# Layer 1's mixer on one Trainium2 core: one Strassen product with 512-column blocks in place of two with 256-column blocks

## The chip, the core and the metric

The kernel runs on one core of a Trainium2 chip. The core has a matrix engine (PE, with its weight loads shown apart as PEld), a vector engine (DVE), a scalar engine (ACT), a general engine (POOL) and a sync engine (SP) that only issues transfers. Operands lie in a memory of 128 partitions; PE writes to eight accumulation banks of 128 x 512 float32 each, which DVE and ACT read. The metric is the device time of one execution in microseconds, lower is better. Before the change it is 975.41 us, the median of three runs (975.31 to 975.7).

## The reference, cut to what matters

Two layers over 512 positions of width 1024. The change lies in the mixer of layer 1:

```python
xn = rms_norm(h, norm_mix[1])
proj = gelu(einsum('bsd,de->bse', xn, w_in_odd[0]))     # 1024 -> 2048
u, v = proj[..., :1024], proj[..., 1024:]
vn = rms_norm(v, sgu_norm)                               # over all 1024 columns of v
gate = einsum('hts,bnshc->bnthc', tril(w_spatial), chunks(vn)) + b_spatial
h = h + einsum('bse,ed->bsd', u * gate, w_out_odd[0])
```

All matrix products are wanted in float32 accuracy.

## The kernel before

**Float32 by three terms.** Every float32 operand is split into a high part `hi` and a rest `lo`, both of the type float32r. A product is `hi*hi + hi*lo + lo*hi`, three matmuls. A weight block is split by `parts` (L149): ACT copies to `hi` (L152), DVE subtracts to `lo` (L153). `summed` (L138) makes `lo` another way: ACT writes the negated copy (L142), a transfer issued by POOL adds the raw weights onto it (L144), and ACT then writes `hi` (L146).

**Buffers.** Raw weights go through four buffers of 128 x 1024 float32 (tag `raw`), which `fetch` (L130) fills from SP's queue (L132). `hi` and `lo` have six buffers of the same size each (tags `whi`, `wlo`). Seven accumulation banks are shared by all products (`mm_bank`), one more (`aux_bank`) by small turns and sums. In the mixer's own pool the tag `vn` has four buffers of 128 x 2048, `v` four of 128 x 1024, `u` two and `ws` one of 128 x 2048.

**The order of instructions.** The program lists instructions in the order of the code; a planner then makes each engine's queue, by priority in that order among what its own cost model says is ready, and gives out buffers in the same pass. So the code of a later step may run ahead of an earlier one. A few instructions are pinned behind the one traced before them on their engine (`inorder`) or behind a named one (`behind`). Once made, each queue is worked off in order, and an instruction that waits holds back all behind it.

**The stage.** `mixer1` (L898) works out 512 positions x 2048 columns from 1024 inputs, in four groups of 512 columns:

1. v's first 512 columns by `v_group` (L905): four position tiles x 8 k blocks x 3 terms, each matmul with a 128 x 128 tile of activations as the stationary operand and a 128 x 512 weight row as the moving one.
2. v's second 512 columns as a Strassen product (Winograd's form), `InProducts("v1", 1536)` (L1045). The activations are cut into halves of positions and of k, the weights into halves of k and of columns (2 x 256). Seven block products take the place of eight. `block_sums` (L946) makes the four sums of activation blocks that products 5, 6, 7 and 3 need; `InProducts.rest` (L992) makes the sums of weight blocks (L995, L997, L999, L1001) and splits them. Each product is, for two position tiles `i`, 4 k blocks x 3 terms (`multiply`, L558, line 581), 128 x 256 wide.
3. u's first 512 columns in the same way, `InProducts("u0", 0)` (L1048).
4. u's second 512 columns by `in_group` (L1145) without Strassen, into which `along` (L1129) weaves the turning of the spatial weights (`turn_spatial`, L1118, whose two turns share the one `aux_bank`), the spatial products (`spatial`, L1069) and the turns of the gated result.

Products gather in banks: 1, 6, 7 and 4 one after the other onto bank `a` of their position tile, 5 and 3 onto bank `e`, 2 in bank `b` (`BANK`, L554). Between them ACT copies the running value out (L1019, L1023), DVE adds the other bank (L1024, L1030), and ACT applies the gelu with the row's norm factor (L1037). In `run` (L1005) the products' order is 1, 1, 2, 2, 6, 6, 5, 7, 5, 7, 4, 3, 4, 3 over the two tiles.

**v's norm.** `v_square` (L931) sums the squares of each half of v by row. `beside_u0` (L1102), run inside u's first product, adds the two sums, takes the inverse root (`newton`, L242, with ACT's root function, L246) and normalises v's first half into `vnh`, `vnl` (`v_normed`, L1053, lines 1058 and 1059, two `vn` buffers). The second half follows after u's first product, into the `vn` buffers that the activation sums held.

Of the kernel before, what the change touches and what calls it, by code (L numbers as in the profile page):

```python
# [8 lines left out]
F32 = mybir.dt.float32  # L9
# [3 lines left out]
ALU = mybir.AluOpType  # L13
PSUM = bass.MemoryType.PSUM

P = 128
# [15 lines left out]
def tile_trunk(ctx: ExitStack, tc: tile.TileContext, x, norm_mix, norm_ffn, final_norm,  # L32
# [3 lines left out]
    nc = tc.nc  # L36
    x = x[0]
# [8 lines left out]
    def mm_bank(name):  # L46
        return ps_mm.tile([P, 512], F32, tag="mm", name=name)
# [82 lines left out]
    def fetch(src, a, b, name):  # L130
        raw = wp.tile([P, a, b], F32, tag="raw", bufs=4, name=f"raw_{name}")
        nc.sync.dma_start(raw, src)  # L132
        return raw, a, b, name
# [124 lines left out]
    def inv_sqrt_cols(ss, n, name):  # L258
        r = tp.tile([P, LINE], F32, tag="rc", name=f"rc_{name}")[:, :n]
        root_ends[name] = inv_sqrt(r, ss, n, name)  # L260
        return r
# [286 lines left out]
    HALF = S // 2  # L548
    NP = NK // 2
# [4 lines left out]
    BANK = {1: "a", 6: "a", 7: "a", 4: "a", 5: "e", 3: "e", 2: "b"}  # L554
# [3 lines left out]
    def multiply(banks, name, product, left, right, both=None):  # L558

        at = BANK[product]
        first = at not in banks
        if first:
            banks[at] = mm_bank(f"{name}{at}")
        ps = banks[at][:, :HALF]
        if both is not None:
            for kp in range(NP):  # L570
                nc.tensor.matmul(banks[at], left(kp)[0], both(kp), start=first and kp == 0,  # L571
                                 stop=kp == NP - 1, skip_group_check=True)
            for kp in range(NP):
                last_matmul[0] = nc.tensor.matmul(ps, left(kp)[1], right(kp)[0], start=False,
                                                  stop=kp == NP - 1, skip_group_check=True)
            return banks[at]
        for kp in range(NP):
            (a_hi, a_lo), (b_hi, b_lo) = left(kp), right(kp)
            for l, r, end in ((a_hi, b_hi, False), (a_hi, b_lo, False),
                              (a_lo, b_hi, kp == NP - 1)):  # L580
                nc.tensor.matmul(ps, l, r, start=first, stop=end, skip_group_check=True)  # L581
                first = False
        return ps
# [314 lines left out]
    def mixer1(norm):  # L898
        w = w_in_odd[0]
        with tc.tile_pool(name="m1", bufs=1) as mp:  # L900
# [27 lines left out]
            banks = v_group(0, {(4, 0): lambda: norm.rstd_cols(inorder)})  # L928
            ssv = mp.tile([P, 4, PAD], F32, name="ssv")[:, :, :NT]

            def v_square(half, t):  # L931
                sq = tp.tile([P, S], F32, tag="sq", name=f"sqv{half}_{t}")
                nc.scalar.activation(sq, v[t][:, half * 512 : (half + 1) * 512], AF.Square,
                                     accum_out=ssv[:, half, t : t + 1])


            sums = [[mp.tile([P, 2, 4, HALF], F32R, name=f"s{q}_{n}", **where)
                     for n, where in enumerate(at)]
                    for q, at in enumerate(((dict(tag="vn", bufs=4),) * 2,
# [22 lines left out]
            def tokens(product, i):  # L962

                def at(kp):
                    if product in SUM:
                        cs = slice(i * P, (i + 1) * P)
                        return tuple(x[:, kp % 2, SUM[product], cs] for x in sums[kp // 2])
                    k = kp if product == 1 else kp + NP
                    cs = slice((i + 2 * (product == 4)) * P, (i + 2 * (product == 4) + 1) * P)
                    return hg[k][0][:, cs], hg[k][1][:, cs]  # L970
                return at

            class InProducts:


                def __init__(self, name, c0):
                    self.name, self.stat = name, {}
                    self.raw = {}
                    for i, j in ((0, 0), (1, 0), (0, 1), (1, 1)):
                        self.raw[i, j] = fetch(  # L980
                            w[i * 512 : (i + 1) * 512, c0 + j * HALF : c0 + (j + 1) * HALF]
                            .rearrange("(k p) c -> p k c", p=P), 4, HALF, f"{name}_{i}{j}")

                def plain(self):
                    self.put(1, parts, (0, 0))
                    self.put(2, summed, (1, 0))

                def put(self, product, how, at):
                    raw, a, b, name = self.raw[at]
                    self.stat[product] = how(raw, a, b, f"{name}_{product}")  # L990

                def rest(self):  # L992
                    b11, b21, b12, b22 = (self.raw[at][0] for at in
                                          ((0, 0), (1, 0), (0, 1), (1, 1)))
                    nc.vector.tensor_tensor(b12, b12, b11, ALU.subtract)  # L995
                    self.put(5, parts, (0, 1))
                    nc.vector.tensor_tensor(b12, b22, b12, ALU.subtract)  # L997
                    self.put(6, parts, (0, 1))
                    nc.vector.tensor_tensor(b11, b12, b11, ALU.subtract)  # L999
                    self.put(7, parts, (0, 0))  # L1000
                    nc.vector.tensor_tensor(b21, b21, b12, ALU.subtract)  # L1001
                    self.put(4, parts, (1, 0))
                    self.put(3, parts, (1, 1))

                def run(self, out_, done, behind_first):  # L1005
                    banks = ({}, {})
                    e = {}
                    for i, product in ((0, 1), (1, 1), (0, 2), (1, 2), (0, 6), (1, 6), (0, 5),
                                       (0, 7), (1, 5), (1, 7), (0, 4), (0, 3), (1, 4), (1, 3)):
                        if (i, product) == (0, 2):  # L1010
                            behind_first()
                        hi, lo = self.stat[product]
                        ps = multiply(banks[i], f"{self.name}_{i}", product, tokens(product, i),
                                      lambda kp: (hi[:, kp, :], lo[:, kp, :]))
                        c = {1: (0, 0), 2: (0, 0), 6: (0, 1), 3: (0, 1), 7: (1, 1), 5: (1, 1),
                             4: (1, 0)}[product]
                        dst = out_(i + 2 * c[0])[:, c[1] * HALF : (c[1] + 1) * HALF]
                        if product in (1, 6):
                            nc.scalar.copy(dst, ps)  # L1019
                        elif product == 5:  # L1020
                            e[i] = ps
                        elif product == 7:
                            nc.scalar.copy(dst, ps)  # L1023
                            nc.vector.tensor_tensor(dst, e[i], dst, ALU.add)  # L1024
                            gelu(dst, dst, i + 2)
                        elif product == 4:
                            gelu(dst, ps, i + 2)
                            done(i + 2)
                        else:
                            nc.vector.tensor_tensor(dst, ps, dst, ALU.add)  # L1030
                        if product == 3:
                            row = out_(i)
                            gelu(row, row, i)
                            done(i)

            def gelu(dst, src, t):
                nc.scalar.activation(dst, src, AF.Gelu, scale=norm.cols[:, t : t + 1])  # L1037
# [3 lines left out]
            v = [mp.tile([P, D], F32, tag="v", bufs=4, name=f"v{t}") for t in range(NT)]  # L1041
            for t in range(NT):
                gelu(v[t][:, :512], banks[t], t)
                v_square(0, t)
            v1 = InProducts("v1", 1536)  # L1045
            v1.plain()
            v1.run(lambda t: v[t][:, 512:], lambda t: v_square(1, t), v1.rest)
            u0 = InProducts("u0", 0)  # L1048
            u0.plain()

            vn, rv = [], []

            def v_normed(half):  # L1053
# [10 lines left out]
            u, gt, mix = {}, {}, {}  # L1064
# [34 lines left out]

            u[0] = mp.tile([P, NT, S], F32, tag="u", bufs=2, name="u0")  # L1100

            def beside_u0():  # L1102
                nc.vector.tensor_tensor(ssv[:, 0, :], ssv[:, 0, :], ssv[:, 1, :], ALU.add)
                rv.append(inv_sqrt_cols(ssv[:, 0, :], NT, "v"))
                v_normed(0)
                u0.rest()

            u0.run(lambda t: u[0][:, t, :], lambda t: None, beside_u0)

            v_normed(1)  # L1110
            ws = wp.tile([P, NK, P], F32, tag="raw", bufs=4, name="ws")
            nc.scalar.dma_start(ws, w_spatial[0].rearrange("h t s -> t h s"))
# [286 lines left out]
    n = mixer0()  # L1399
    n = ffn0(n)  # L1400
    n = mixer1(n)
    ffn1(n)

# [29 lines left out]
```

## Time and profile before

| what | value |
|---|---|
| median of three runs | 975.41 us |
| the profiled execution's span | 973.0 us |
| mean granted PE clock | 0.998 |
| v's first half (v_group), start | 485.29 us |
| the two Strassen products, first to last start | 508.00 to 548.24 us |
| u's second half, start | 548.36 us |
| output projection (oo), start | 578.47 us |

Times are counted from the span's start. The span runs from the first to the last instruction of one profiled execution. A row of a timeline has the start, the duration, the engine, the line, the operation and the tiles as out<-in, their shape, the count of merged instructions and, in brackets, how long the engine was idle before it and what ended that. The duration of one matmul is longer than the step to the next, since matmuls are pipelined; the pace is read from start to start. Windows list each engine's busy time with the number of instructions, the granted clock, the share of the transfer engines and their rate.

### The profile page before, as it was taken

The page shows a single profiled execution, that of the slowest core. Times are in us where ns is not written, and L with a number is a line of the kernel's source. Part 1 is how long each engine was busy: PE and PEld are TensorE (multiplying, and loading weights), DVE is VectorE, ACT ScalarE, POOL GpSimd, SP SyncE. Part 2 cuts the span into 40 slices and gives each one's busy share as a digit, 9 for nine tenths or more (in the row PEclk, how much of TensorE's full clock was granted, in tenths as well). Part 3 has the DMA queues.
Part 4 walks back from the last instruction along what each step waited for, and adds up shares of the span by engine and source line. Part 5 has one row for each costly group of instructions (what it writes and reads, how often), then busy time and mean ns, then how long its engine had stood idle before and what let it go on. Part 6 is the DMA issues. An engine that isn't in the chain of part 4 may idle for free.

```text
span 973.0 us, 14003 instructions
## 1 busy us (share of the span) xinstructions
PE 963.6 (99%) x5120; PEld 828.8 (85%) x5120; DVE 817.0 (84%) x1393; ACT 598.7 (62%) x905; POOL 149.9 (15%) x173
## 2 busy tenths in 40 slices
PE   9999999999999999999999999999999999999996
PEld 7888888988888888888889988889888888888885
DVE  5887458999899898998986865589998989889897
ACT  5523347765676665765487734587765667656775
POOL 2142023110111010110310001221111011100123
PEclk9999999999999999999999999999999999999999
DMA  7442225776777677774324623167767777668775
GB/s 251 146 139 86 87 88 108 178 178 165 195 178 181 146 178 185 174 174 140 119 58 110 221 67 99 55 132 187 186 145 194 196 173 172 156 165 201 194 153 140
DMA packets 94417, 148.36 MB, mean 152 GB/s; under 512 B 5156, under 2 KB 60428, under 8 KB 94348
## 3 DMA queue, kind: packets, MB, share of 16 engines
q1 hardware_dynamic: 78316, 98.69, 32.2%
q0 software_dynamic: 14256, 46.93, 26.7%
q10 hardware_dynamic: 1776, 1.84, 0.6%
q8 instruction: 40, 0.66, 0.3%
q14 instruction: 29, 0.24, 0.1%
HBM read 98.42 MB, written 2.10 MB: 103 GB/s over the span
## 4 chain that ended last, share of the span: by engine, by line
PE 99%; DVE 1%; issue 0%; ACT 0%; POOLq 0%; DVEq 0%; POOL 0%
PE dn L158 3%; PE d L158 3%; PE dn L159 3%; PE dn L157 3%; PE d L159 3%; PE d L157 3%; PE gu L157 2%; PE gu L159 2%; PE oo L159 1%; PE oo L157 1%; PE gu L158 1%; PE oe L157 1%; PE oe L159 1%; PE oo L158 1%; PE oe L158 1%; PE u_2a L581 1%
## 5 line engine op out<-in xcount | busy, mean ns | idle before, releaser
L617 DVE SCALAR_TENSOR_TENSOR c<-rows,prm,c 128x512 f32<-128x512 f32 x88 | 65.6, 748 | 1.5 <-ACT c L615 1.4
L144 POOL DMA_DIRECT2D wlo_g<-raw_g x20 | 17.2, 860 | 321.3 <-DVE kept L804 187.4
L158 PE MATMUL dn<-wlo_dn,a_hi 128*128 128x512 f32 x144 | 56.3, 391 | 0.0
L158 PE MATMUL d<-a_lo,whi_d 128*128 128x512 f32 x144 | 56.3, 391 | 0.0
L159 PE MATMUL dn<-whi_dn,a_lo 128*128 128x512 f32 x144 | 56.2, 391 | 0.0
L159 PE MATMUL d<-a_hi,wlo_d 128*128 128x512 f32 x144 | 56.2, 390 | 0.0
L157 PE MATMUL d<-a_hi,whi_d 128*128 128x512 f32 x144 | 56.2, 390 | 0.0
L157 PE MATMUL dn<-whi_dn,a_hi 128*128 128x512 f32 x144 | 56.2, 390 | 0.0
L731 ACT ACTIVATE whi_a<-raw_g 128x512 fp32r<-128x512 f32 x20 | 12.6, 631 | 61.0 <-PE g_10e L571 8.7
L213 POOL TENSOR_TENSOR ssq_f<-ssq_f,sq_f 128x512 f32<-128x512 f32 x14 | 19.8, 1411 | 134.4 <-ACT sq_f L212 99.5
L202 ACT ACTIVATE hg<-h,prm 128x512 fp32r<-128x512 f32 x24 | 17.3, 722 | 34.9 <-DVE h L315 34.9
L142 ACT ACTIVATE wlo_g<-raw_g 128x1024 fp32r<-128x1024 f32 x20 | 21.2, 1062 | 27.5 <-PE g_2e L581 8.8
L615 ACT ACTIVATE c<-rows,prm 128x512 f32<-128x512 f32 x44 | 31.3, 715 | 6.6 <-DVE rows L828 6.6
L1187 DVE SCALAR_TENSOR_TENSOR y<-dn,small,y 128x512 f32<-128x512 f32 x40 | 28.0, 749 | 8.6 <-PE dn L159 8.6
L625 ACT ACTIVATE s<-c,prm 128x512 f32<-128x512 f32 x44 | 31.4, 715 | 6.2 <-DVE c L617 6.1
L203 DVE SCALAR_TENSOR_TENSOR hg<-h,prm,hg 128x512 fp32r<-128x512 f32 x24 | 23.6, 986 | 11.1 <-ACT hg L202 11.1
L266 ACT ACTIVATE a_hi<-s 128x512 fp32r<-128x512 f32 x40 | 24.9, 627 | 11.4 <-PE d L159 7.7
L159 PEld LDWEIGHTS dn<-whi_dn,a_lo 128*128 128x128 f32 x144 | 27.1, 188 | 5.7
L159 PEld LDWEIGHTS d<-a_hi,wlo_d 128*128 128x128 f32 x144 | 27.1, 188 | 5.6
L153 DVE TENSOR_TENSOR wlo_dn<-raw_dn,whi_dn 128x1024 fp32r<-128x1024 f32 x18 | 22.0, 1224 | 11.7 <-ACT whi_dn L152 11.7
L157 PEld LDWEIGHTS dn<-whi_dn,a_hi 128*128 128x128 f32 x144 | 27.1, 188 | 5.3
L157 PEld LDWEIGHTS d<-a_hi,whi_d 128*128 128x128 f32 x144 | 27.1, 188 | 5.3
(1132 smaller groups left out, 3319.9 us busy)
## 6 DMA issues: line engine op xcount, KB each, us to landing
raw_g<-in_w_ffn_gate_dram SPq DMA_DIRECT2D x40, 512.0 KB, 3.8
raw_u<-in_w_ffn_up_dram SPq DMA_DIRECT2D x40, 512.0 KB, 4.0
raw_dn<-in_w_ffn_down_dram SPq DMA_DIRECT2D x22, 512.0 KB, 6.3
wlo_u<-raw_u POOLq DMA_DIRECT2D x21, 512.0 KB, 6.1
wlo_g<-raw_g POOLq DMA_DIRECT2D x20, 512.0 KB, 4.6
raw_d<-in_w_ffn_down_dram SPq DMA_DIRECT2D x18, 512.0 KB, 4.2
wlo_s12g<-s12g POOLq DMA_DIRECT2D x18, 512.0 KB, 6.3
wlo_s34g<-s34g POOLq DMA_DIRECT2D x18, 512.0 KB, 5.5
```

Source lines behind the costliest of these rows:

```text
L142: first = nc.scalar.activation(lo, raw, AF.Copy, scale=-1.0)
L153: behind(nc.vector.tensor_tensor(lo, raw, hi.bitcast(F32), ALU.subtract), after[0])
L157: nc.tensor.matmul(ps, lhs[0], rhs[0], start=start, stop=False)
L158: nc.tensor.matmul(ps, lhs[0], rhs[1], start=False, stop=False)
L159: nc.tensor.matmul(ps, lhs[1], rhs[0], start=False, stop=stop)
L203: nc.vector.scalar_tensor_tensor(hg[k][1], h[k], g, hg[k][0].bitcast(F32), op0=ALU.mult, op1=ALU.subtract)
L213: nc.gpsimd.tensor_tensor(self.ssq, self.ssq, sq, ALU.add)
L266: nc.scalar.activation(hi, src, AF.Copy, scale=scale)
L615: nc.scalar.activation(c, t[:, 0:S], AF.Copy, scale=prm("cf", ft))
L617: self.last_conv = nc.vector.scalar_tensor_tensor(c, t[:, i : S + i], prm("cf", i * NF + ft), c, op0=ALU.mult, op1=ALU.add)
L625: self.last_silu = nc.scalar.activation(s, c, AF.Silu, bias=self.prm("bf", ft))
L1187: return nc.vector.scalar_tensor_tensor(dst, ps, ffn.cols[:, t : t + 1], dst, op0=ALU.mult, op1=ALU.add)
```

## The change

The second 512 columns of v (columns 1536 to 2047 of the weights) and the first 512 of u (columns 0 to 511) become the left and the right column half of one Strassen product, whose weight blocks are 512 rows x 512 columns. Each weight block is now handled in two chunks of 2 k blocks x 512 columns, the same size as a former block. v's blocks are fetched in four chunks through the `raw` buffers; u's two blocks come by one transfer each into two of the four `vn` buffers (`across`). The order is by product, both position tiles of each: 1, 2, 5, 6, 7, 4, 3. The first 256 positions of v are complete after product 2, the others after product 4; the first 256 of u after product 3, the others after product 7. `rest` is hooked in front of product 2, and the norm of v with the normalisation of its first half (`v_whole`) in front of product 3.

```diff
+            across = {at: mp.tile([P, 4, 512], F32, tag="vn", bufs=4, name=f"raw_vu_{at[0]}{at[1]}")
+                      for at in ((0, 1), (1, 1))}
             sums = [[mp.tile([P, 2, 4, HALF], F32R, name=f"s{q}_{n}", **where)
...
-                def __init__(self, name, c0):
...
+                def __init__(self, name, c0, c1):
+                    self.name, self.stat, self.raw = name, {}, {}
+                    for i in range(2):
+                        self.raw[i, 0] = [
+                            fetch(w[(4 * i + 2 * n) * P : (4 * i + 2 * n + 2) * P, c0 : c0 + 512]
+                                  .rearrange("(k p) c -> p k c", p=P), 2, 512,
+                                  f"{name}_{i}0_{n}")[0] for n in range(2)]
+                    for i in range(2):
+                        t = across[i, 1]
+                        nc.sync.dma_start(t, w[i * 512 : (i + 1) * 512, c1 : c1 + 512].rearrange(
+                            "(k p) c -> p k c", p=P))
+                        self.raw[i, 1] = [t[:, 2 * n : 2 * n + 2, :] for n in range(2)]
...
                 def put(self, product, how, at):
-                    raw, a, b, name = self.raw[at]
-                    self.stat[product] = how(raw, a, b, f"{name}_{product}")
+                    self.stat[product] = [how(raw, 2, 512, f"{self.name}_{product}_{n}")
+                                          for n, raw in enumerate(self.raw[at])]
+
+                def less(self, to, x, y):
+                    for n in range(2):
+                        nc.vector.tensor_tensor(self.raw[to][n], self.raw[x][n], self.raw[y][n],
+                                                ALU.subtract)
 
                 def rest(self):
...
+                    b11, b21, b12, b22 = (0, 0), (1, 0), (0, 1), (1, 1)
+                    self.less(b12, b12, b11)
+                    self.put(5, parts, b12)
+                    self.less(b12, b22, b12)
+                    self.put(6, parts, b12)
+                    self.less(b11, b12, b11)
+                    self.put(7, parts, b11)
+                    self.less(b21, b21, b12)
+                    self.put(4, parts, b21)
+                    self.put(3, parts, b22)
+
+                def multiply(self, banks, i, product):
+                    at = BANK[product], i
+                    first = at not in banks
+                    if first:
+                        banks[at] = mm_bank(f"{self.name}_{at[0]}{i}")
+                    left = tokens(product, i)
+                    for kp in range(NP):
+                        lhs = left(kp)
+                        rhs = [x[:, kp % 2, :] for x in self.stat[product][kp // 2]]
+                        for l, r, end in ((0, 0, False), (0, 1, False), (1, 0, kp == NP - 1)):
+                            nc.tensor.matmul(banks[at], lhs[l], rhs[r], start=first, stop=end,
+                                             skip_group_check=True)
+                            first = False
+                    return banks[at]
+
+                def run(self, dst, done, hooks):
+                    banks = {}
+                    for product in (1, 2, 5, 6, 7, 4, 3):
+                        for i in range(2):
+                            if (product, i) in hooks:
+                                hooks[product, i]()
+                            ps = self.multiply(banks, i, product)
+                            if product == 5:
+                                continue
+                            t = i + 2 * (product in (7, 4))
+                            d = dst[product in (6, 7, 3)](t)
+                            if product in (1, 6, 7):
+                                nc.scalar.copy(d, ps)
+                            if product in (2, 7, 3):
+                                nc.vector.tensor_tensor(d, banks["e", i] if product == 7 else ps,
+                                                        d, ALU.add)
+                            if product in (2, 7, 3):
+                                gelu(d, d, t)
+                            elif product == 4:
+                                gelu(d, ps, t)
+                            if product in (2, 4):
+                                done(t)
...
-            v1 = InProducts("v1", 1536)
-            v1.plain()
-            v1.run(lambda t: v[t][:, 512:], lambda t: v_square(1, t), v1.rest)
-            u0 = InProducts("u0", 0)
-            u0.plain()
...
-            def beside_u0():
+            vu = InProducts("vu", 1536, 0)
+            vu.plain()
+
+            def v_whole():
                 nc.vector.tensor_tensor(ssv[:, 0, :], ssv[:, 0, :], ssv[:, 1, :], ALU.add)
                 rv.append(inv_sqrt_cols(ssv[:, 0, :], NT, "v"))
                 v_normed(0)
-                u0.rest()
-
-            u0.run(lambda t: u[0][:, t, :], lambda t: None, beside_u0)
-
+
+            vu.run([lambda t: v[t][:, 512:], lambda t: u[0][:, t, :]], lambda t: v_square(1, t),
+                   {(2, 0): vu.rest, (3, 0): v_whole})
             v_normed(1)
```

More of the change, by code (lines that the diff above doesn't have):

```diff
@@ L973, in mixer1 @@
             class InProducts:
-                def __init__(self, name, c0):
[L977 to L982, printed above, removed]
+                def __init__(self, name, c0, c1):
[10 more added lines that the diff above has]
+                        self.raw[i, 1] = [t[:, 2 * n : 2 * n + 2, :] for n in range(2)]
                 def plain(self):
@@ L988, in put @@
                 def put(self, product, how, at):
-                    raw, a, b, name = self.raw[at]
-                    self.stat[product] = how(raw, a, b, f"{name}_{product}")
-                def rest(self):
[L993 to L1034, printed above, removed]
```

## The prediction

> **What bounds the kernel now.** I read the page's busy times first, then the shares of the chain of waits, then everything that the matmul engine waited for in the whole span.
>
> ```profile
> span 973.0 us, 14003 instructions
> PE 963.6 (99%) x5120; PEld 828.8 (85%) x5120; DVE 817.0 (84%) x1393; ACT 598.7 (62%) x905; POOL 149.9 (15%) x173
> ...
> PE 99%; DVE 1%; issue 0%; ACT 0%; POOLq 0%; DVEq 0%; POOL 0%
> ```
> ```profile
> PE clock L61 <- DVE idle L56: 1.3, 1, 1.3
> PE z L441 <- ACT hg L409: 0.3, 1, 0.3
> ```
>
> PE is busy for 99% of the span, the chain is 99% PE, and its waits (us, times, longest) come to 1.6 us, all at the start of the kernel. So a saving reaches the end only if PE's stream gets shorter, and any other engine costs something only where it makes PE wait for the first time. A PE that is "busy" may still be slow, so the next view is its pace: start to start of neighbouring matmuls, in the timeline and in the window of the two products.
>
> ```profile
> 485.29 0.39 PE L157 MATMUL v<-whi_v,hg 128*128 128x512 f32 x1
> ...
> 495.94 0.39 PE L159 MATMUL v<-whi_v,hg 128*128 128x512 f32 x1
> ```
> ```profile
> core 0: us, PE busy (x) PEld busy (x), PEclk, DMA share, GB/s
> 508.00:548.36 40.36, 40.36 (x336) 40.32 (x335) 1.00 0.52 154
> ```
>
> The first fence is the first and the 48th matmul of v's first half, 512 columns wide: 47 steps in 10.65 us, 226.6 ns each. The second holds the two Strassen products, 256 columns wide: 336 matmuls in 40.36 us, 120.1 ns each, at a granted clock of 1.00 and with no hole. Two narrow steps are 240.2 ns, 13.6 ns more than a wide one. From 256 to 512 columns a step grows by 106.5 ns; so 120.1 - 106.5 = 13.6 ns belong to the instruction, not to its columns.
>
> **The change part by part.**
>
> *PE.* Removed: 2 x 7 products x 2 token tiles x 4 k blocks x 3 terms = 336 matmuls of 256 columns, 40.36 us. Added: half as many, 168, of 512 columns: 168 x 226.6 ns = 38.07 us. Term: -2.29 us. It is the only one with work on the critical engine.
>
> The Trainium skill, "TensorE: Matmul & The Clock Gate", section "Back-to-back issue gap", gives N/2.4 + 2.5 ns for an isolated stream of N columns, hence a fixed part of 2.5 ns where these rows show 13.6; by it the saving would be an estimated 168 x 2.5 ns = 0.42 us. The trace disagrees with both of its paces (109.2 and 215.8 ns by the rule), so the rows decide.
>
> *Weights and their splits.* Data volume, the number of 128x1024 splits (14) and that of 128x1024 subtractions (8) are unchanged; the first two operands of each block are only cut into two chunks. With a product every 24 x 226.6 ns = 5.44 us from 508.0, the starts are: 1 at 508.0, 2 at 513.4, 5 at 518.9, 6 at 524.3, 7 at 529.8, 4 at 535.2, 3 at 540.6, and u's second half at 546.1. Each product now takes two of the six hi/lo buffers, so three products fit instead of six; in time that is 3 x 5.44 = 16.3 us instead of 6 x 2.88 = 17.3 us, nearly the same lead. A buffer pair is free two products before its next user starts, 10.9 us, and a pair of splits needs about 1.06 + 2 x 1.22 = 3.5 us by these rows:
>
> ```profile
> 503.80 1.06 ACT L152 ACTIVATE whi_v<-raw_v 128x1024 fp32r<-128x1024 f32 x1
> ...
> 504.90 1.22 DVE L153 TENSOR_TENSOR wlo_v<-raw_v,whi_v 128x1024 fp32r<-128x1024 f32 x1
> 506.04 1.22 DVE L999 TENSOR_TENSOR raw_v<-raw_v,raw_v 128x1024 f32<-128x1024 f32 x1
> 507.17 1.22 DVE L1001 TENSOR_TENSOR raw_v<-raw_v,raw_v 128x1024 f32<-128x1024 f32 x1
> ```
>
> Cost 0, hidden under the two products in between; without that cover, 3.5 us per product.
>
> *Ahead of 508.0.* VectorE is the tight engine there:
>
> ```profile
> core 0: us, PE busy (x) PEld busy (x) DVE busy (x) ACT busy (x) POOL busy (x), PEclk, DMA share, GB/s
> 484.00:508.00 24.00, 24.00 (x112) 19.99 (x110) 23.02 (x36) 18.40 (x23) 4.62 (x4) 1.00 0.18 45
> 508.00:528.20 20.20, 20.20 (x170) 20.20 (x169) 11.84 (x15) 15.05 (x30) 0.86 (x1) 1.00 0.47 132
> 528.20:548.40 20.20, 20.20 (x170) 20.20 (x170) 16.66 (x25) 19.61 (x35) 1.10 (x1) 1.00 0.56 176
> ```
>
> It is 23.02 of 24 us busy, but of that three subtractions (L997, L999, L1001) and two splits, 5 x 1.22 = 6.1 us, now belong to products 5, 6 and 7, which start at 518.9 or later; the second chunk of product 1 adds 1.22. The window after it has 8.4 us of VectorE to spare. Product 2's low half goes through two accumulating transfers instead of one (the second of the two was u's); its second buffer comes free when v's first half is through its second chunk, 485.3 + 2 x 5.44 = 496.2, and after a 1.06 us copy and a landing like that of the loads below, 4.6 us, it is there near 502 and needed at 513.4. Cost 0.
>
> *The two 1 MB loads* that now hold the u columns sit behind the four chunk loads on SP's queue, and their tiles come free when the layer before ends:
>
> ```profile
> 467.72 10.51 SPq L132 DMA_DIRECT2D raw_v<-in_w_in_odd_dram  x4
> 508.47 34.13 SPq L132 DMA_DIRECT2D raw_u<-in_w_in_odd_dram  x8
> ```
> ```profile
> DMA to landing us min/median/max: 4.3/4.6/4.7
> ```
>
> SP has nothing to issue from 478.2 to 508.5, so nobody is queued behind them. Four times 512 KB at 4.6 us is 18.4 us at worst: from 485.3, where the layer before ends, to 503.7, and the window 484 to 508 moves only 45 GB/s. First use is 518.9 less 3.5. Cost 0. The other bound: begun only at 508, the second load would land at 526.4 and product 6 start 3.5 us later, 5.6 us late; the free queue speaks against it.
>
> *Draining the banks.* Copies and adds become half as many and twice as wide, a little cheaper in sum, off the path. What changes is the cover: bank "a" is copied out by ScalarE after products 6 and 7 and written again by the next product's same tile, with one 12-matmul block, 2.72 us, in between instead of two narrow ones, 2.88 us. The wide copy by the nearest row is 0.60 us:
>
> ```profile
> 511.13 0.38 ACT L1019 COPY v<-v_0a 128x256 f32<-128x256 f32 x1
> 511.38 1.08 ACT L152 ACTIVATE whi_v<-raw_v 128x1024 fp32r<-128x1024 f32 x1
> 512.34 0.38 ACT L1019 COPY v<-v_1a 128x256 f32<-128x256 f32 x1
> ...
> 567.07 0.69 ACT L1037 ACTIVATE u<-u,rc_m1c 128x512 f32<-128x512 f32 x1 [1.51 <-PE u L159]
> 567.74 0.60 ACT L1096 ACTIVATE mx<-mT 128x512 fp32r<-128x512 f32 x1
> ```
>
> Behind two splits it would be 2.12 + 0.60 + about 0.3 for the handover = 3.0 us, 0.3 too late, at four places. Bounds 0 and 1.2 us; I take 0, since the rows at 511 to 512 show copies put between the splits as they fall due.
>
> *v's norm moves.* Now v's last columns come from product 4, at 540.6, not 528; the sum of squares, the root and the normalisation of v's first half leave product 1-3 of u and land at the border to u's second half.
>
> ```profile
> 531.92 0.63 ACT L933 ACTIVATE sqv<-v 128x512 f32<-128x512 f32 x1
> 532.45 0.19 ACT L933 ACTIVATION_READ_ACCUMULATOR sqv<-v 128x1 f32 x1
> ...
> 533.88 1.28 ACT L246 ACT_TABLE_LOAD   x1
> 535.18 0.20 ACT L246 ACTIVATE sd_v<-ms_v 128x4 f32<-128x4 f32 x1
> ...
> 536.40 2.57 ACT L1058 ACTIVATE vnh<-v,rc_v 128x512 fp32r<-128x512 f32 x4
> ...
> 539.38 2.01 ACT L152 ACTIVATE whi_u<-raw_u 128x1024 fp32r<-128x1024 f32 x2
> ...
> 543.45 1.28 ACT L1037 ACT_TABLE_LOAD   x1
> ...
> 551.85 0.58 ACT L1125 ACTIVATE wsT<-wst 128x512 fp32r<-128x512 f32 x1
> ```
> ```profile
> 553.12 0.69 DVE L1126 TENSOR_TENSOR wsT<-wst,wsT 128x512 fp32r<-128x512 f32 x1
> ```
> ```profile
> 554.31 0.60 PE L1121 MATMUL wst<-ident,ws 128*128 128x128 f32 x4
> ...
> 560.24 0.39 PE L157 MATMUL sp<-vnh,wsT 128*128 128x512 f32 x1
> ```
>
> From the last read of squares to the first vnh it takes 536.40 - 532.64 = 3.8 us. After product 4: 0.3 handover, gelu 0.69 and square 0.82, then 3.8: vnh from 546.2 to 548.8. Its user, the spatial product, stands 11.9 us behind the start of u's second half (560.24 - 548.36), so at 558.0: 9 us of cover. Cost 0, with the rivals below for when it is not.
>
> Sum: -2.29 us on the profiled execution's own time, span 973.0, giving 970.7. Around the span lie 975.41 - 973.0 = 2.4 us that the change does not touch, so against the median: **973.1 us**, 0.23% less.
>
> **The rivals.** A difference of 0.2%, 1.95 us, is about what a measurement of this kernel can tell from none: below 973.46 is faster, above 977.36 slower.
>
> *The transposes' bank.* The two turns of the spatial weights share one bank; the second, 5.95 us after the start of u's second half (554.31 - 548.36), waits until ScalarE and VectorE have read the first. Before, it was read at 551.85 and by VectorE in 0.69 us from 553.12, 0.5 us ahead of need. Now vnh ends at 548.8, a table load and two gelus take 1.28 + 1.4, the second half's vnh 2.6, then 0.58 and 0.69 for the reads: 555.4, against a need at 552.0: 3.4 us late if all of that is queued first, nothing if the reads go first. 974.1 to 976.5, in the middle 975.3. For it: the order puts what was traced earlier first. Against: PE's own order is made with these times in view, and can take the next matmuls ahead of the turn.
>
> *Slower: u's second-half splits end up behind the norm.* Before, its first splits ran at 539.38, 9 us early. ScalarE was 19.61 of 20.2 us busy there; if the splits fall behind vnh, the first chunk is ready at 548.8 + 1.06 + 1.22 = 551.1 instead of 546.1, 5.0 us of idle PE: 978.1. It costs the gain from 2.29 us of idling on and shows as slower from 4.24 on. Against: the buffers for it come free at 535.2, 10.9 us early, when the norm cannot run yet.
>
> *Pace.* If the wide matmuls of a Strassen product took the pair's 240.2 ns (the weight loads fill 40.32 of 40.36 us now), nothing is gained: 975.4. Against: v's first half has the same kind of operands and makes 226.6. By the rule of the Trainium skill cited above, the time would be an estimated 975.0.
>
> **How the numbers follow.** Forecast 0.55; the transposes' bank 0.17; the splits behind the norm 0.17; pace 0.03; 0.08 for a new order elsewhere in the stage that I don't see, mostly slower. Faster: the forecast less its upper edge, 0.54. Same: bank, pace and that edge, 0.22. Slower: 0.24. The forecast alone reaches from 972.4 to 974.3: down by 0.7, since each of the some dozen interruptions of u's second half costs PE about 0.09 us (after a turn the next step is 0.32 instead of 0.23) and their order is made anew; up by the 1.2 of the bank copies. For 8 in 10 the range goes up into the slower case: 972.4 to 977.6.
>
> ```profile
> 551.47 0.48 PE L157 MATMUL u<-whi_u,hg 128*128 128x512 f32 x1
> 551.79 0.39 PE L158 MATMUL u<-wlo_u,hg 128*128 128x512 f32 x1
> ```
>
> **What would show it.** Right: 168 wide matmuls in 38.1 us without a hole, u's second half starting at about 546.1, PE's waits still 1.6 us, and the span near 970.7. Each step fails visibly: a pace above 227 ns; a PE wait on the copy of bank "a" at a product's border; on the turned spatial weights near 552; on u's splits at 546; on the subtraction behind the 1 MB loads near 519. Above all a second-half start later than 548.4 would make the prediction wrong.

## The result and the profile after

The changed kernel takes 972.68 us (median of 12 runs, 972.59 to 973.59), the kernel before 975.13 us in 12 runs beside it (974.23 to 975.7). The ratio is 0.9976 with a 95% interval of 0.9968 to 0.9985: 2.45 us faster, and by the interval between 1.5 and 3.1 us. The forecast was 973.1 us against 975.41, a gain of 2.29; so the total alone could not tell 2.29 from half a microsecond more or less, and the trace has to. In the profiled executions the span went from 973.0 to 970.9; the forecast was 970.7.

The page of the changed kernel, then the window of the one Strassen product (columns as in the window before: busy time and count of PE and of its weight loads, granted clock, share and rate of transfers):

```profile
span 970.9 us, 13658 instructions
PE 961.0 (99%) x4952; PEld 818.6 (84%) x4952; DVE 812.9 (84%) x1387; ACT 597.5 (62%) x895; POOL 152.0 (16%) x173
```
```profile
508.08:546.18 38.10, 38.10 (x168) 31.27 (x167) 1.00 0.32 106
```

This window ends 0.05 us before the next matmul starts (546.23). Counted up to that start, as the 40.36 us of the two products before are, 168 matmuls take 38.15 us, 227.1 ns each. That is the whole gain: -2.21 us of the forecast -2.29. The weight loads, which filled 40.32 of 40.36 us before, are now busy for 31.27 of 38.10. From PE's timeline, the first matmul of the product, the first of u's second half and the first of the output projection:

```profile
508.08 0.39 PE L1026 MATMUL vu_a<-whi_vu,hg 128*128 128x512 f32 x1
...
546.23 0.39 PE L157 MATMUL u<-whi_u,hg 128*128 128x512 f32 x1
...
576.36 0.39 PE L157 MATMUL oo<-mx,whi_oo 128*128 128x512 f32 x1
```

The product starts 0.08 us later than before; u's second half starts 2.13 us earlier (548.36 before) and the output projection 2.11 earlier (578.47 before). The lead stays to the end: the span is 2.1 us shorter. So nothing was given back between the product and the last instruction. PE's waits in the whole span are these:

```profile
PE clock L61 <- DVE idle L56: 1.3, 1, 1.3
PE z L441 <- ACT hg L409: 0.3, 1, 0.3
PE g_10a L571 <- DVE rows L804: 0.3, 1, 0.3
PE u_10a L571 <- DVE kept L804: 0.2, 1, 0.2
```

The two new ones, 0.5 us together, are not in the changed stage but in the FFN; in a second profile of the same kernel they are absent and the span is 970.3, so they are the scatter of single executions.

What moved is the norm of v. ScalarE's timeline at the border, and PE's beside it:

```profile
543.04 0.19 ACT L933 ACTIVATION_READ_ACCUMULATOR sqv<-v 128x1 f32 x1
544.59 0.72 ACT L1055 ACTIVATE u<-u,rc_m1c 128x512 f32<-128x512 f32 x1 [1.36 <-DVE u L1045]
545.33 1.28 ACT L246 ACT_TABLE_LOAD   x1
...
547.80 1.28 ACT L1055 ACT_TABLE_LOAD   x1
549.10 0.72 ACT L1055 ACTIVATE u<-u,rc_m1c 128x512 f32<-128x512 f32 x1
549.73 5.00 ACT L1070 ACTIVATE vnh<-v,rc_v 128x512 fp32r<-128x512 f32 x8
554.63 0.57 ACT L1139 ACTIVATE wsT<-wst 128x512 fp32r<-128x512 f32 x1
```
```profile
548.96 0.60 PE L1135 MATMUL wst<-ident,ws 128*128 128x128 f32 x4
...
556.51 0.66 PE L1135 MATMUL wst<-ident,ws 128*128 128x128 f32 x4
...
558.16 0.39 PE L157 MATMUL sp<-vnh,wsT 128*128 128x512 f32 x1
```

All eight normalisations run in one piece from 549.73, in front of the first read of the turned weights at 554.63. PE's second turn, which stood 5.95 us behind the start of u's second half, now stands 10.3 us behind it (556.51 - 546.23): the planner let matmuls of u go ahead. That is the constellation of the first rival, and it cost PE nothing here.

### The profile page after: what moved, and what is told of

Its sections match the earlier page's. It is cut to its first block, busy times and chain, and to the rows that moved or that the text cites. A ratio compares the mean times of both kernels' runs of the same rounds, so it can differ in the third digit from the quotient of the medians.

```text
span 970.9 us, 13658 instructions
## 1 busy us (share of the span) xinstructions
PE 961.0 (99%) x4952; PEld 818.6 (84%) x4952; DVE 812.9 (84%) x1387; ACT 597.5 (62%) x895; POOL 152.0 (16%) x173
## 4 chain that ended last, share of the span: by engine, by line
PE 94%; DVE 3%; DMA 1%; issue 1%; ACT 0%; POOLq 0%; DVEq 0%; POOL 0%
PE dn L158 3%; PE dn L159 3%; PE dn L157 3%; PE d L158 3%; PE d L157 3%; PE d L159 3%; PE vu_a L1026 2%; PE gu L157 2%; PE gu L159 2%; PE oo L159 2%; PE oo L157 2%; PE gu L158 2%; PE oe L159 1%; PE oe L158 1%; PE oo L158 1%; PE oe L157 1%
## 5 line engine op out<-in xcount | busy, mean ns | idle before, releaser
L158 PEld LDWEIGHTS dn<-wlo_dn,a_hi 128*128 128x128 f32 x144 | 27.0, 188 | 5.4
```

Of the source, the lines that this page charges most:

```text
L158: nc.tensor.matmul(ps, lhs[0], rhs[1], start=False, stop=False)
```

## The experiments

All kernels below start from the changed one unless said otherwise. The kernel before ran beside each on the same chip and gave 974.7 to 975.0 us.

### Is the gain the cost of an instruction?

```diff
-                            nc.tensor.matmul(banks[at], lhs[l], rhs[r], start=first, stop=end,
-                                             skip_group_check=True)
-                            first = False
+                            for cs in (slice(0, 256), slice(256, 512)):
+                                nc.tensor.matmul(banks[at][:, cs], lhs[l], rhs[r][:, cs],
+                                                 start=first, stop=end, skip_group_check=True)
+                                first = False
```

A first form gave each half a start flag of its own, and leaves out part of the sums:

> The changed kernel with each 512-column matmul of the one Strassen product cut into two of 256 columns side by side; all else as changed. Theory (the gain is the fixed 13.6 ns of 168 instructions fewer): the product takes 336 x 120.1 ns = 40.35 us instead of 38.10, the span 970.9 + 2.25 = 973.1, and against the kernel before the ratio is 1.000. Rival (the gain comes from the new order, the merged loads or fewer copies and adds): the ratio stays near 0.9976.

The form of the diff has one flag for the bank. The changed kernel itself ran beside it:

> The changed kernel with each 512-column matmul of the one Strassen product cut into two of 256 columns, with one start flag for the whole bank. Theory: the product takes 40.35 us, the ratio to the kernel before is 1.000 within 0.001. Rival (the gain is from the new order, loads or fewer copies): 0.9976.

> The changed kernel itself, beside the narrow one on the same chip. Theory: ratio 0.9976 to the kernel before, 2.3 us below the narrow one; a product stage of 38.1 us.

The first form took 974.7 us, ratio 0.9999 (0.9990 to 1.0008), span 973.6. The second took 974.71 us, ratio 1.0000 (0.9991 to 1.0009). The changed kernel took 972.18 us on that chip, ratio 0.9974 (0.9964 to 0.9984). The timeline of the second form, the product's first row and the first of u's second half:

```profile
508.16 0.40 PE L1027 MATMUL vu_a<-whi_vu,hg 128*128 128x256 f32 x2
...
548.47 0.40 PE L157 MATMUL u<-whi_u,hg 128*128 128x512 f32 x1
```

The product takes 40.31 us again, 120.0 ns a matmul, 2.16 us more than in the changed kernel. With the new order, the merged loads, the fewer copies and the late norm all in place (the normalisations start at 551.65 here, 3.2 us behind the start of u's second half, in the changed kernel 3.5), nothing of the gain is left. So the gain is that of the 168 instructions fewer, and the rest of the change is worth 0 within 0.1%. Every matmul comes with a weight load of its own, and of these too there are 168 fewer (4952 for 5120); the run does not tell which of the two holds the 13.6 ns.

### What sets a step: the instruction, the columns or the weight load?

```diff
-                    mm3(banks[j], (hg[k][0][:, cs], hg[k][1][:, cs]), chunks[k],
-                        i == 0, i == NK - 1)
+                    cuts = ((0, 512),) if i < 2 else ((0, 256), (256, 512)) if i < 4 else (
+                        (0, 384), (384, 512)) if i == 5 else tuple((c, c + 128) for c in range(0, 512, 128))
...
+                        for c0, c1 in cuts:
+                            nc.tensor.matmul(banks[j][:, c0:c1], l, r[:, c0:c1],
...
```

> The changed kernel with v's first half, per k block in PE's order, as 512; 512; 2 x 256; 2 x 256; 4 x 128; 384 + 128; 4 x 128; 4 x 128 columns, all adjacent. Theory (13.6 ns per instruction plus 0.416 ns per column): steps of 120 ns at 256, 67 ns at 128, 173 ns at 384, and the stage longer by 24 x 13.6 + 12 x 13.7 + 36 x 41 ns = 2.0 us. Rival (a narrow step is set by its weight load, so it does not fall below the 120 ns seen at 256): 120 ns at 128 columns, 36 x 253 + 12 x 66 + 24 x 13.6 ns = 10.2 us longer.

In the one execution of this kernel the stage ran from 485.08 to 521.46, 36.4 instead of 22.7 us: 13.7 longer, more than either theory gave. Rows of the timeline at each width (the 256, the 384 + 128 and the 128 columns), each with the start of its neighbour:

```profile
495.79 0.40 PE L930 MATMUL v<-wlo_v,hg 128*128 128x256 f32 x2
496.03 0.40 PE L930 MATMUL v<-whi_v,hg 128*128 128x256 f32 x2
...
510.16 0.45 PE L930 MATMUL v<-wlo_v,hg 128*128 128x384 f32 x2
510.45 0.90 PE L930 MATMUL v<-whi_v,hg 128*128 128x384 f32 x6
511.18 0.61 PE L930 MATMUL v<-wlo_v,hg 128*128 128x128 f32 x4
...
516.99 1.05 PE L930 MATMUL v<-whi_v,hg 128*128 128x128 f32 x8
517.88 0.61 PE L930 MATMUL v<-wlo_v,hg 128*128 128x128 f32 x4
```

256 columns: 0.240 us for two, 120 ns a step. 384 + 128: 0.29 us from one pair to the next (510.16 to 510.45); the row at 510.45 merges one more pair with the first four matmuls of 128 columns, and start by start the trace has 287 ns a pair. 128: 0.89 us for eight, 111 ns a step. So the straight line of the theory (67 ns at 128) breaks below 256 columns; there is a floor of 111 ns, of the same size as the rival's 120 but below it. The eight matmuls of one column from 496.27 to 497.08 bear it out: behind the first, they too step by 111 to 113 ns. That fits a weight load that takes some 111 ns of pace, but the run does not separate it from another limit per instruction. Two things follow for the change. At 256 columns the floor is 9 ns away, so the step of 120 there is not the floor itself. And in the mixed pair the narrow matmul pays the floor too: 287 ns is close to the theory's 173 for 384 columns plus 111, 284, and not to 512 columns plus two fixed parts, 240. The Trainium skill, "TensorE: Matmul & The Clock Gate", section "LDWEIGHTS (loading the stationary operand)", gives columns / 1.2 ns for a load, an estimated 106.7 ns for 128; the 111 ns stand near it.

The rest of the 13.7 us is the clock. Windows of the same run, over the first and the second part of the first 128-column stretch, most of the 384 + 128 stretch, and its end with the start of the last 128-column stretch (PE busy, granted clock, share and rate of transfers):

```profile
497.08:499.35 2.27, 2.27 (x22) 1.00 0.00 0
499.35:505.48 6.13, 6.13 (x32) 0.53 0.34 64
505.48:510.16 4.68, 4.68 (x21) 0.52 0.77 145
510.16:513.00 2.84, 2.84 (x27) 1.00 0.00 0
```

From 499.35 to 510.16 the granted clock was 0.53 and 0.52, and a step of 128 columns took 213 ns. If every step were longer there by as much as the clock is lower, that would lose 6.13 x 0.47 + 4.68 x 0.48 = 5.1 us. Floor and extra instructions make 36 x (4 x 111.3 - 226.6) + 24 x 13.6 + 12 x (287 - 226.6) ns = 8.9 us; the two together are 14.0, a little above the 13.7. The steps at the lower clock are not quite twice as long (213 ns against 111 for 128 columns, 0.53 us against 0.29 for a pair).

### Is the late norm hidden only by PE's order?

In the first four k blocks of u's second half every matmul is pinned behind the one traced before it:

```diff
-            mm3(banks[j], lhs(ks[i], j), rhs(ks[i], j), i == 0, i == len(ks) - 1)
+            mm3(banks[j], lhs(ks[i], j), rhs(ks[i], j), i == 0, i == len(ks) - 1,
+                inorder if name == "u1" and i < 4 else lambda ins: ins)
```

> The changed kernel with PE's order in the first four k blocks of u's second half kept as the code has it, so that the second turn of the spatial weights stands 5.95 us behind the start as in the kernel before. Theory (the late norm is hidden only because PE's order lets matmuls go ahead of the turn): the turn, ready at 556.5 in the changed kernel, stalls PE from 552.1 by up to 4.4 us; at least 1 us, as ScalarE and VectorE can be ordered anew, so 973.7 to 977. Rival (the norm has cover anyway): within 0.3 us of 972.7.

> The control: the same pin in the kernel before, whose order in that place already is the code's. Both theories: no change, ratio 1.000 within 0.0005.

Pinned, the changed kernel takes 977.32 us, ratio 1.0026 (1.0016 to 1.0036), 4.6 us more than unpinned; the kernel before takes 974.78, ratio 1.0002 (0.9993 to 1.0011). PE's waits of the pinned kernel, and its timeline and windows at the place:

```profile
PE sp L157 <- ACT wsT L1140: 3.0, 1, 3.0
```
```profile
551.59 0.39 PE L159 MATMUL u<-whi_u,hg 128*128 128x512 f32 x1
554.94 0.50 PE L157 MATMUL sp<-vnh,wsT 128*128 128x512 f32 x1 [2.95 <-ACT wsT L1140]
```
```profile
551.60:555.00 3.40, 0.45 (x3) 1.00 0.00 0
555.00:558.50 3.50, 3.50 (x11) 0.57 0.00 0
```

The step from 551.59 to 554.94 is 3.1 us too long: PE waits for ScalarE's read of the first turn, which stands behind eight normalisations in this kernel too. Right after it the granted clock falls to 0.57 for 3.5 us, which costs 1.5 more; together 4.6. So the late read behind the norm, from which the first rival starts, is real, and only PE's order keeps it from the time. The wait fell on the spatial product, which needs the turned weights themselves, and held up the turn behind it; I had it fall on the turn first, for the shared bank.

### How thick is that cover?

```diff
                 v_normed(0)
+                (hi, lo) = vn[0]
+                for t in range(NT):
+                    src = v[t][:, :512]
+                    nc.scalar.activation(hi[:, t, :], src, AF.Copy, scale=rv[0][:, t : t + 1])
+                    nc.vector.scalar_tensor_tensor(lo[:, t, :], src, rv[0][:, t : t + 1],
...
```

> The changed kernel with the normalisation of v's first half done twice over (the same values written again), which adds 4 x 0.63 us on ScalarE and 4 x 0.66 us on VectorE right at the border to u's second half. In the changed kernel VectorE's last read of the turned weights that the first spatial product needs ends at 556.46, and the product starts at 558.16: 1.7 us of cover. Theory (the cover is that thin, but PE's order lets u's matmuls go ahead of the spatial products): between 972.7 and 973.7. Rival (the border has room enough, as the prediction's 9 us of cover say): 972.7, no matmul's place changed. Other rival (the order cannot give way): 972.7 + 2.6 - 1.7 = 973.6 or more, with a PE wait on the turned weights or on vnl.

972.82 us, ratio 0.9980 (0.9970 to 0.9989): no loss that can be told, and span 971.0. But the order changed: PE's timeline shows the second turn in the middle of the spatial products.

```profile
558.71 0.39 PE L158 MATMUL sp<-vnl,wsT 128*128 128x512 f32 x1
558.94 0.62 PE L1142 MATMUL wst<-ident,ws 128*128 128x128 f32 x4
559.32 0.94 PE L159 MATMUL sp<-vnh,wsT 128*128 128x512 f32 x3
```

The turn slid from 10.3 to 13 us behind the start, and the spatial products' third terms slid behind it. It is the theory's case at its lower end. The rival that the border has 9 us of room falls by the order alone, since places changed; the time would suit it too.

### What covers the two large loads?

The two 1 MB loads are issued ahead of v's four chunk loads:

```diff
+                    for i in range(2):
+                        t = across[i, 1]
+                        last = nc.sync.dma_start(t, w[i * 512 : (i + 1) * 512, c1 : c1 + 512]
...
+                            behind(nc.sync.dma_start(
+                                raw, w[(4 * i + 2 * n) * P : (4 * i + 2 * n + 2) * P, c0 : c0 + 512]
...
```

> The changed kernel with the two 1 MB loads of u's weight blocks put ahead of v's four chunk loads on SP's queue instead of behind them. Their tiles come free only when the layer before ends, at 485.6 in the changed kernel, so v's chunks then start at 486.5 at the earliest instead of by 478. Theory (their place at the end of the queue is the cover): 2 MB at the 244 GB/s of the window 485 to 496 land by 494.5, v's first chunk by 497, the fourth by 503.5; product 1 can still be split by 508, product 2's low half, made by copy and transfer (1.04 + 4.6 us), is at 509 and due at 513.5: 0 to 2 us lost, 972.7 to 974.7. Rival (there is slack for it): within 0.3 us of 972.7.

976.25 us, ratio 1.0014 (1.0004 to 1.0024), 3.6 us more than the changed kernel: the direction of the theory, and nearly twice its upper end. PE's waits, and the time to landing of the six loads:

```profile
PE vu_b L1030 <- DMA wlo_vu<-raw_vu: 1.9, 2, 1.5
...
PE vu_a L1030 <- DVE wlo_vu L153: 0.5, 1, 0.5
PE vu_a L1030 <- ACT whi_vu L152: 0.4, 1, 0.4
```
```profile
DMA to landing us min/median/max: 4.6/8.9/12.8
```

PE waits 2.8 us in products 1 and 2, and the steps at these waits are 4.0 us too long in all. What I had left out: ScalarE, whose order then put the gelus of v's first half before the splits, made product 2's negated copy only at 510.8 and 512.7 instead of 500.1 and 503.0. With the order that follows from it, the chunks' place at the head of the queue is worth 3.6 us; in the changed kernel they have it.

### The same idea in the FFN

```diff
-    FIRST_WIDE = {"g": 4, "u": 6}
+    FIRST_WIDE = {"g": 4, "u": 4}
```

> The same idea taken to the FFN: in the fifth hidden block pair (f = 4) of both layers, u's products 1, 6, 7 and 4 as four matmuls of 512 columns (high and low half side by side) and four of 256 instead of twelve of 256; each of these products then needs one more add on VectorE. Theory (a matmul costs 13.6 ns plus its columns): 4 x 13.6 ns less for 4 products in 2 layers, -0.43 us, 972.25, if the adds are hidden. Rival (VectorE, 23.5 of 25 us busy there, cannot take 8 adds more): 972.7 or more, with PE waiting on VectorE's adds.

With `"g": 2` instead of 4 as well:

> The same once more, from the block pair before on (f = 2): there g's seven products and u's products 2, 5 and 3 too. Theory: 14 products in each of 2 layers, 28 x 54 ns = -1.5 us against the changed kernel, 971.2, if the adds are hidden. Rival (the adds are not hidden, VectorE being 18.7 of 20 us busy in that stage): slower than the changed kernel, with PE waiting on VectorE.

982.64 us, ratio 1.0082 (1.0066 to 1.0097), and 996.98 us, ratio 1.0231 (1.0216 to 1.0246). Both expectations of a gain miss; the rivals have the direction. In the first, PE's longest waits are:

```profile
PE g_10e L574 <- DMA wlo_s12g<-s12g: 2.1, 1, 2.1
PE g_10a L571 <- DVE rows L804: 2.0, 1, 2.0
```

They lie at f = 10, three block pairs behind the edit, where the changed kernel waits 0.3 us; in the window 250 to 300 us PE is busy for 45.81 us at a clock of 0.97, where the changed kernel has 49.53 at 1.00:

```profile
250.00:300.00 50.00, 45.81 (x236) 0.97 0.69 166
```

The wider matmuls save less than expected: in the first layer u's products 1, 6, 7 and 4 at f = 4 take 5.61 us instead of 5.75 by their steps, 36 ns a product where 54 were forecast, since a step of 512 columns is 232 ns there. The waits name VectorE's sums and an accumulating transfer; why these come late was not followed up. How much of the 10 us is the eight adds and how much the new order was not separated. In the second kernel the longest waits stand nearer to the edit, at f = 4 and 6, and are for ScalarE's splits of weights, not straight for VectorE as the rival had it; ScalarE itself waited 2.34 us for VectorE shortly before (at 192.41), and what part that has was not followed up:

```profile
PE g_4a L571 <- ACT whi_s12g L764: 5.3, 2, 2.9
PE g_6b L571 <- ACT whi_g L146: 4.3, 1, 4.3
```

No other kernel here is faster than the changed one.

## Why the prediction was right, point by point

- **The pace.** Right: 227.1 ns for 226.6, -2.21 us for -2.29. (A pace above 227 ns was named as a sign of being wrong; 227.1 stands just past it and is worth 0.08 us, and the second profile has 226.9.) The narrow form shows that nothing else in the change makes the gain, the widths show that 256 columns lie above the floor. The rule of the Trainium skill for an isolated stream, weighed there with 0.42 us, does not hold for these matmuls: both its paces are some 11 ns below the rows, before and after.
- **Weights and splits.** Right in the size of the lead: u's first split ran at 534.73, 11.5 us before its use, where the estimate was 10.9 (the buffers free at 535.2). The slower rival needed these splits behind the norm; the order had them before it, so it did not come about.
- **Ahead of 508.0.** Right: the start moved by 0.08 us, VectorE was busy for 19.43 of the 24 us instead of 23.02. Product 2's second transfer was issued at 504.31, later than the estimate of about 497, and in time.
- **The two loads.** Cost 0, as taken, by their place at the end of the queue; the reversed order cost 3.6 us.
- **Draining the banks.** Taken as 0 with an upper bound of 1.2. One of the four places was used up: ScalarE copied product 6's second tile at 531.84, and the wait list of PE's weight loads has the wait for it; PE itself did not wait.

```profile
PEld vu_a L1026 <- ACT u L1043: 0.2, 1, 0.2
```

- **v's norm.** The cost of 0 held, the reason did not. The prediction had the normalisation from 546.2 to 548.8 and 9 us of cover. It ran from 549.73. From the last read of squares (543.04 to 543.23) to the first vnh it takes 6.5 us, not 3.8: the prediction did not count that ScalarE waits 1.36 us for VectorE's sum of u, nor that two gelus of u, a split and a load back to the gelu come in between. Nor did it count in its cover that both halves' normalisations run together and delay the read of the turned weights to 554.63. The cover that was left is 1.7 us, from the end of VectorE's read at 556.46 in the row below to the spatial product at 558.16, and it exists because PE's order was made anew. The prediction has this only as the argument against its first rival, not in its term of 0; that the term came out so is in part luck. Pinned, the same lateness costs 4.6 us, above the rival's 3.4: the wait itself was 3.1, and the fall of the clock behind it was not in the sum.

```profile
555.78 0.68 DVE L1140 TENSOR_TENSOR wsT<-wst,wsT 128x512 fp32r<-128x512 f32 x1
```

## What to carry to other kernels

Where PE is dense, count its instructions: at the same number of columns streamed, a matmul of 512 columns instead of two of 256, with one weight load less, saved about 13 ns here, and that can be read off beforehand as the difference of two rates of start to start. Read them off at the place itself: in the FFN the same step gave some 9 ns. A rebuild for it must keep PE dense: work that moves to a border can be hidden by the matrix engine's own order, so look at the order after the change before trusting a cover computed from the order before. And a wait of 3 us costs more than itself, if the clock falls behind it.

## What the runs showed of the hardware that was not expected

- A step of 128 columns takes 111 ns at full clock, not 67, and one of a single column as long; 256 columns take 120. So below 256 columns a narrower matmul is hardly faster. Beside one of 384 columns it costs the same: 287 ns a pair.
- The granted clock can fall although PE waits for nothing: to 0.53 and 0.52 over 10.8 us in the run of widths, about 3 us after eight matmuls of one column (which every kernel here has, without a fall) and then the first 128-column stretch began. Narrow matmuls alone do not make it fall: the last 128-column stretch of the same run, from 510.73 to 521.46, kept a clock of 1.00. What did is open.
- Behind the pinned kernel's wait of 3.1 us the clock was 0.57 over 3.5 us, 0.50 from 555.48 to 558.89. In the FFN run with `"g": 2` it fell to 0.50 at the end of each of the three longest waits or just behind it: for 3.4 us at each of the two of g_4a (5.3 us in all), and for 10.2 us at the one of 4.3 us of g_6b. The Trainium skill, "TensorE: Matmul & The Clock Gate", section "What's actually happening", tells of an idle window of about 3.4 us after which the clock is halved; the halving and the length of the shorter falls agree, but some of these waits were shorter than that window, and in the run of widths PE did not wait.
